# Broadcasting RMS-norm factors in a transposed decoder trunk: two DMAs through a scratch row, and sums as two single products of 132 columns

## The chip, the cores and the metric

One core of a Trainium2 chip runs the kernel. The metric is the device time of one launch in microseconds (us); lower is better. The engines of a core work side by side: TensorE (PE, matrix products, with its weight load PEld), VectorE (DVE), ScalarE (ACT), GpSimd (POOL) and SyncE (SP, which issues most weight transfers). DMA engines move data between HBM, SBUF (on-chip memory, 128 partitions) and the scratch rows in HBM. Products land in PSUM, eight banks of 128 x 512 f32.

## What is computed

A decoder trunk of two layers over 256 tokens of width 1024, all in f32, with a memory of 256 entries. Each layer is FFN, mixer, FFN; layer 0 mixes with an mLSTM, layer 1 with sliding-window attention, and both have four heads of attention to the memory beside it.

```python
def rms_norm(x, g):
    return x * lax.rsqrt(jnp.mean(x * x, axis=-1, keepdims=True) + EPS) * g

mem_kv = rms_norm(mem, mem_norm_g) @ mem_w_kv
for i in range(2):
    x = x + 0.5 * swiglu(rms_norm(x, ffn1_norm_g[i]), ffn1_w_in[i], ffn1_w_out[i])
    proj = rms_norm(x, mix_norm_g[i]) @ (a_w_in, b_w_in)[i]
    x = x + jnp.concatenate([token_mixer(proj), memory_heads(proj)], axis=-1) @ w_out
    x = x + 0.5 * swiglu(rms_norm(x, ffn2_norm_g[i]), ffn2_w_in[i], ffn2_w_out[i])
```

There are seven norms of this kind: one of the memory, and x0 to x5 of the activations. The factor `rsqrt(mean + EPS)` is one number per token.

## The kernel before

**Layout.** Activations lie transposed: channels on the partitions, the 256 tokens along the columns. An activation is four tiles of 128 x 2 x 256. Weights come in tiles of 128 x 1024 (512 KB) by SP's queue into `wr` (five buffers). Each f32 product is made as three faster ones: ACT casts a weight tile to its high part `wh` (L211), DVE subtracts to get the low part `wl` (L212), eight buffers each, and `mm3` issues high x high, low x high and high x low (L225 to L227). A group of 512 output columns fills one PSUM bank.

**Norms.** The gain of a norm is applied before the product (`split_gain` makes `xh` and `xl`, L241 the DVE half), the token factor behind it, so that the products of the next stage run before the factor is known. The squares are added up in `acc` by DVE (L288, folded in L291). `Norm.chain` then makes the factor. Two products on PE with `acc` as the stationary operand and a column of ones as the moving one give the token sums in two columns of a bank (L231 through `mmf`); `rsqrt_cols` makes mean + EPS on DVE (L250) and the power -0.5 on POOL (L251): `rc`, 128 x 2, one token per partition. Where tokens lie along the columns, the factor must stand in every partition: `bcast_rows` (two products with the identity, L231 again) and an ACT copy give `rb`, 128 x 256 (L306), and another `hrb`, half of it. An f32 product takes two passes on PE, so the trace counts four for two products. `rows=False` (the memory norm and x4, the norm before the attention mixer) needs only `rc`.

**Who uses them.** `rb` scales the FFN's hidden units on DVE (L476, followed by a Silu on ACT), in mixer A the output gates (L658), the gate pre-activations (L696, L697) and queries and keys (L754, L757). `hrb` scales the FFN's output (L544, in the last FFN also L533). `rc` scales the columns of groups whose tokens lie on the partitions: through `head_scales` (`qsc`, L364, L365) it goes to `head_norm`, which makes the norm of each head: a square on ACT, a reduce (L374), L377, the power on POOL (L379), L381 and the scaling L383. So in the memory stage and in mixer B, keys and queries wait for `rc`. In the memory stage the second of two key heads is transposed on PE at L236.

**Order.** The program runs memory, FFN, mixer A, FFN, FFN, mixer B, FFN. The order on PE and SP is written out by hand by `Weave`: the main line issues weight products and moves a virtual clock by the price of each; side chains such as `Norm.chain` are spawned with a delay from the table `LAT` and take their turn when the clock has passed it. `LAT['norm_b']` is the delay between the sums and the broadcast, `x0_b` the same for x0. The order on the other engines (DVE, ACT, POOL) is decided by the framework from what becomes ready when; a DMA issued by POOL stands in POOL's queue, and a wait there holds back what is behind it. The late constants, the mask among them, are loaded by POOL's queue (L183 to L190). Mixer A already sends a scratch row through HBM (`gd`, L710, L713), on ACT's queue.

Of the kernel before, what the change touches and what calls it, by code (L numbers as in the profile page):

```python
# [10 lines left out]
F32 = mybir.dt.float32  # L11
# [3 lines left out]
AF = mybir.ActivationFunctionType  # L15
ALU = mybir.AluOpType
# [3 lines left out]
P = 128  # L20
T = 256
D = 1024
# [10 lines left out]
def constants():  # L33
# [16 lines left out]

LAT = dict(pieces=1, norm=7.5, norm_b=4.8, mnorm=2.4, x0=16.0, x0_b=7.5, mkeys=7.2, cross=9.5, cross_s=1.5,
           cross_m=3.7, cross_p=8.7, cross_o=3.0, gates=20.0, scores=2.2, scores_m=8.4, num=6.9, num_r=7.5,
           keys=5.5, keys_d=7.2, query=9.0, head=1.5, head_m=2.5, head_p=9.3, head_o=4.0)


WARM = 18


class Weave:
# [37 lines left out]
def tile_trunk(ctx: ExitStack, tc: tile.TileContext, a, out):  # L99
    nc = tc.nc  # L100
    seq = [0]

    def mk(pool, shape, dt, tag):
        seq[0] += 1
        return pool.tile(shape, dt, tag=tag, name=f"{tag}_{seq[0]}")

    def pool(name, bufs, **kw):
        return ctx.enter_context(tc.tile_pool(name=name, bufs=bufs, **kw))
# [13 lines left out]
    sp = pool("sp", 2)  # L122
# [8 lines left out]
    def act(*args, **kw):  # L131
        ins = nc.scalar.activation(*args, **kw)  # L132
        if args[2] not in (AF.Copy, AF.Square):
            tabled[0] = ins
# [12 lines left out]
    def col():  # L147
        return mk(cp, [P, 16], F32, "col")

    def mo():  # L150
        return mk(pb8, [P, 512], F32, "bank")
# [15 lines left out]
    ident = con[:, C_ID:C_ID + P]  # L167
    maskd = con[:, C_MASK:C_MASK + T]
    ones = mk(cst, [P, 1], F32, "ones")
# [33 lines left out]
    pieces = [1]  # L203
# [26 lines left out]
    def mmf(ps, lhsT, rhs, n, start=True, stop=True):  # L230
        nc.tensor.matmul(ps, lhsT, rhs, start=start, stop=stop, skip_group_check=True)  # L231
        wv.now += max(0.213, n * 0.00182)
# [15 lines left out]
    def rsqrt_cols(dst, src, n, scale):  # L248
        c = col()
        nc.vector.tensor_scalar(c[:, :n], src, scale, EPS, op0=ALU.mult, op1=ALU.add)  # L250
        nc.gpsimd.tensor_tensor(out=dst, in0=c[:, :n], in1=mhalf[:, :n], op=ALU.pow)  # L251

    def bcast_rows(ps, cols):
        for h in range(2):
            mmf(ps[:, h * P:(h + 1) * P], cols[:, h:h + 1].to_broadcast([P, P]), ident, P)

    def pair(x):
        return x.unsqueeze(1).to_broadcast([P, 2, T])


    class Norm:
# [30 lines left out]

        def chain(self, gap=LAT['norm_b']):
            pc = mo()
            for h in range(2):
                mmf(pc[:, h:h + 1], self.acc[:, 0, h * P:(h + 1) * P], ones, 1)
            self.rc = mk(sp, [P, 2], F32, "rc")
            rsqrt_cols(self.rc, pc[:, 0:2], 2, 1.0 / D)
            if not self.rows:
                self.done = True  # L300
                return
            yield gap
            ps = mo()
            bcast_rows(ps, self.rc)
            self.rb = mk(sp, [P, T], F32, "rb")
            nc.scalar.copy(self.rb, ps[:, :T])  # L306
            if self.half:
                self.hrb = mk(sp, [P, T], F32, "hrb")
                act(self.hrb, ps[:, :T], AF.Copy, scale=0.5)
            self.done = True  # L310

        def ready(self):
# [55 lines left out]
    def head_norm(dst, src, n, hsc):  # L368

        hd = src.shape[2] // n  # L370
        sq, v, u = tmp(), col(), col()
        sqv = sq[:, :, :n * hd]
        act(sqv, src, AF.Square)
        nc.vector.tensor_reduce(out=v[:, 0:2 * n].rearrange("p (h m) -> p h m", h=2),  # L374
                                in_=sqv.rearrange("p h (m d) -> p h m d", m=n), axis=AX.X, op=ALU.add)
        for h in range(2):
            nc.vector.tensor_scalar(u[:, n * h:n * h + n], v[:, n * h:n * h + n], hsc[:, h:h + 1], EPS,  # L377
                                    op0=ALU.mult, op1=ALU.add)
        nc.gpsimd.tensor_tensor(out=u[:, 8:8 + 2 * n], in0=u[:, 0:2 * n], in1=mhalf[:, 0:2 * n], op=ALU.pow)  # L379
        for h in range(2):  # L380
            nc.vector.tensor_scalar(v[:, 8 + n * h:8 + n * h + n], u[:, 8 + n * h:8 + n * h + n],  # L381
                                    hsc[:, 2 + h:3 + h], None, op0=ALU.mult)
        tt(out=dst.rearrange("p h (m d) -> p h m d", m=n), in0=src.rearrange("p h (m d) -> p h m d", m=n),  # L383
           in1=v[:, 8:8 + 2 * n].rearrange("p (h m) -> p h m", h=2).unsqueeze(3).to_broadcast([P, 2, n, hd]),
           op=ALU.mult)
# [12 lines left out]
    x0 = Norm(G_F1)  # L398

    def memory():  # L400
# [3 lines left out]
        bank = mo()  # L404
        for i in range(WARM):
            nc.tensor.matmul(bank, idle[:, :P], idle, start=True, stop=True, skip_group_check=True)
# [16 lines left out]
        def keys(gi, kr):  # L423
            nc.scalar.copy(kT[gi], turn(kr))
            return
            yield

        for gi in range(2):
# [13 lines left out]
            norm.fold()  # L442
            wv.spawn(norm.chain(), LAT['mnorm'])
            gv = Group(wkv, 512, mh, ml, rows=True)
# [5 lines left out]
            for i, q in enumerate((first, gr)):  # L450
                kr = tmp()
                head_norm(kr, q.ps, 2, hsc)
                wv.spawn(keys(i, kr), LAT['mkeys'] + 1.5 * i)
        for gi in range(2):
# [7 lines left out]
            if gi == 0:  # L462
                with tc.issue_after(last[0].ins):
                    for c2 in range(4):
                        x0.put(xT[c2])
                wv.spawn(x0.chain(LAT['x0_b']), LAT['x0'])

# [41 lines left out]
    def ffn(x, w_in, w_out, nxt=None, mid=None):  # L509
# [13 lines left out]
        for c2 in range(4):  # L523
            wts = [(kg, w[:, kg[0]:kg[0] + kg[1], c2 * 256:(c2 + 1) * 256]) for kg in KG]
            if nxt is None and c2 == 3:
                wts = [(kg, wtile(src, kg[1])) for kg, src in wts]
                y = tmp()
                for m in range(2):
                    ps = mo()[:, :T]
                    for kg, wt in wts:  # L530
                        products(ps, m, kg, wt, True)
                        yield
                    tt(out=y[:, m], in0=ps, in1=x.hrb, op=ALU.mult)  # L533
                    tt(out=y[:, m], in0=y[:, m], in1=x.xT[c2][:, m], op=ALU.add)
                    nc.scalar.dma_start(out[:, 2 * c2 + m], y[:, m])
                return
            ps = mo()
            for kg, src in wts:
                wt = wtile(src, kg[1])
                for m in range(2):  # L540
                    products(ps[:, m * T:(m + 1) * T], m, kg, wt, m == 0)
                    yield
            t = tmp()
            tt(out=t, in0=halves(ps), in1=pair(x.hrb), op=ALU.mult)  # L544
            xn = unit(F32)
            tt(out=xn, in0=t, in1=x.xT[c2], op=ALU.add)
            if nxt is None:
                nc.scalar.dma_start(out[:, 2 * c2:2 * c2 + 2], xn)
            else:
                nxt.put(xn)  # L550
        wv.spawn(nxt.chain(), LAT['norm'])

# [15 lines left out]
    def cross_spawn(gr, gi, layer, hsc, ys):  # L568
# [4 lines left out]
        def queries():  # L573
# [4 lines left out]
            for m in range(2):  # L578
                wv.spawn(head(m), LAT['cross_s'] + LAT['cross_m'] * m)
            return  # L580
            yield

        def head(m):
            hd, qT = gi * 2 + m, cell[0]
            hi, lo = ys.tiles(4 + gi)
            s = mo()
            for h in range(2):
                mmf(s[:, h * T:(h + 1) * T], qT[:, m, h * P:(h + 1) * P], kT[gi][:, m], T)
            sv = halves(s)
            c = col()  # L590
            nc.vector.tensor_reduce(out=c[:, 2:4], in_=sv, axis=AX.X, op=ALU.max, negate=True)  # L591
            p = unit(F32)
            for h in range(2):
                act(p[:, h], sv[:, h], AF.Exp, bias=c[:, 2 + h:3 + h], accum_out=c[:, 4 + h:5 + h])
            nc.vector.reciprocal(c[:, 6:8], c[:, 4:6])
            tt(out=p, in0=p, in1=c[:, 6:8].unsqueeze(2).to_broadcast([P, 2, T]), op=ALU.mult)
            yield LAT['cross_p']
            tps = mo()
            for mc in range(2):
                for h in range(2):  # L600
                    transpose(tps[:, mc * T + h * P:mc * T + (h + 1) * P], p[:, h, mc * P:(mc + 1) * P])
            pT = tmp()
            nc.scalar.copy(pT, halves(tps))
            yield LAT['cross_o']
            o = mo()
            for mc in range(2):
                mmf(o[:, :T], vM[:, mc, hd * P:(hd + 1) * P], pT[:, mc], T, mc == 0, mc == 1)
            split_plain(o[:, :T], hi[:, m], lo[:, m])
            ys.done.add(8 + hd)
# [39 lines left out]
    def mixer_a(x, nxt):  # L649
# [6 lines left out]
        def og_out(gr):  # L656
            t = unit(F32)
            tt(out=t, in0=gr.ps, in1=pair(x.rb), op=ALU.mult)  # L658
            act(t, t, AF.Sigmoid)
            og.append(t)  # L660
# [366 lines left out]
```

## Time and profile before

| | |
|---|---|
| median of three runs | 1012.32 us (1012.27 to 1013.65) |
| profiled execution | 1012.23 us, span of its trace 1010.4 us |
| granted TensorE clock | 1.000 |
| DMA | 182.70 MB, mean 181 GB/s |
| DVE weight splits `wl` (L212) | x347, 414.7 us busy |
| ACT weight casts `wh` (L211) | x347, 356.8 us busy |
| POOL | 32 instructions, 35.7 us busy |

A row of the timeline view reads: start in us, length in us, engine, line, operation, what is written from what, shapes, number of instructions run together; in brackets the idle time of the engine before it and what ended that. L225 and so on are lines of the kernel before. A group row of the page reads: line, engine, operation, tiles, shapes and count, then busy us and mean ns of one, then idle time of the engine before them with what ended most of it.

### The profile page before, as it was taken

How to read it: one execution, taken by the hardware profiler on the slowest of the kernel's cores; microseconds unless marked ns; L12 is line 12 of the kernel's file. 1: busy time of each engine (PE TensorE's matmuls, PEld its weight loads, DVE VectorE, ACT ScalarE, POOL GpSimd, SP SyncE). 2: the span in 40 equal slices, each digit the busy share in tenths (PEclk: the TensorE clock that was granted, in tenths of full speed). 3: DMA queues.
4: the chain of work that ended last, by engine and by line, in shares of the span. 5: the costliest groups of instructions: out<-in, count | busy, mean ns of one | idle time of the engine just before them, and what ended most of it. 6: DMA issues, size and time to landing. Idle time of an engine off the chain costs nothing.

```text
span 1010.4 us, 20624 instructions
## 1 busy us (share of the span) xinstructions
PE 998.5 (99%) x8594; PEld 980.2 (97%) x8594; DVE 655.5 (65%) x1063; ACT 519.5 (51%) x764; POOL 35.7 (4%) x32
## 2 busy tenths in 40 slices
PE   8999999999999999999999999999999999999998
PEld 7999999999999999999999999999987899999998
DVE  6866665577856676665558666656787766666551
ACT  7754445446656554444445544544557754454440
POOL 1200000000001000000000000000121000000000
PEclk9999999999999999999999999999999999999999
DMA  9776656666644566665676666567541347666550
GB/s 308 242 245 200 192 180 185 199 183 179 184 139 133 167 210 195 200 189 170 192 206 205 189 191 201 173 197 198 182 131 66 100 131 220 198 189 185 188 170 21
DMA packets 173204, 182.70 MB, mean 181 GB/s; under 512 B 7124, under 2 KB 168328, under 8 KB 173112
## 3 DMA queue, kind: packets, MB, share of 16 engines
q1 hardware_dynamic: 171872, 179.60, 58.3%
q10 hardware_dynamic: 1016, 1.58, 0.5%
q8 instruction: 67, 1.10, 0.5%
q0 software_dynamic: 224, 0.22, 0.2%
q14 instruction: 25, 0.20, 0.1%
HBM read 180.32 MB, written 1.05 MB: 180 GB/s over the span
## 4 chain that ended last, share of the span: by engine, by line
PE 94%; DVE 3%; ACT 1%; DMA 1%; POOL 0%; issue 0%; SPq 0%; ACTq 0%
PE bank L225 30%; PE bank L226 30%; PE bank L227 30%; PE bank L231 2%; PE bank L236 1%; ACT u L132 1%; DVE wl L212 1%; DMA wr<-in_mem_w_kv_dram 1%; PE bank L961 1%; POOL col L379 0%; DVE col L930 0%; DVE u L383 0%; DVE col L591 0%; PE bank L925 0%; DVE u L946 0%
## 5 line engine op out<-in xcount | busy, mean ns | idle before, releaser
L212 DVE TENSOR_TENSOR wl<-wr,wh 128x1024 fp32r<-128x1024 f32 (+1 forms) x347 | 414.7, 1196 | 279.8 <-ACT wh L211 279.0
L211 ACT CAST wh<-wr 128x1024 fp32r<-128x1024 f32 (+1 forms) x347 | 356.8, 1031 | 393.1 <-PE bank L226 368.9
L225 PE MATMUL bank<-xh,wh 128*128 128x256 f32 x1544 | 429.1, 278 | 0.0
L226 PE MATMUL bank<-xl,wh 128*128 128x256 f32 x1544 | 426.8, 276 | 0.0
L227 PE MATMUL bank<-xh,wl 128*128 128x256 f32 x1544 | 426.8, 276 | 0.0
L226 PEld LDWEIGHTS bank<-xl,wh 128*128 128x128 f32 x1544 | 290.3, 188 | 0.1
L225 PEld LDWEIGHTS bank<-xh,wh 128*128 128x128 f32 x1544 | 290.0, 188 | 0.1
L227 PEld LDWEIGHTS bank<-xh,wl 128*128 128x128 f32 x1544 | 289.9, 188 | 0.0
L225 PE MATMUL bank<-u,wh 128*128 128x256 f32 x896 | 249.3, 278 | 0.0
L226 PE MATMUL bank<-u,wh 128*128 128x256 f32 x896 | 247.6, 276 | 0.0
L227 PE MATMUL bank<-u,wl 128*128 128x256 f32 x896 | 247.6, 276 | 0.0
L225 PEld LDWEIGHTS bank<-u,wh 128*128 128x128 f32 x896 | 168.2, 188 | 1.9 <-issue 1.7
L226 PEld LDWEIGHTS bank<-u,wh 128*128 128x128 f32 x896 | 168.4, 188 | 0.1
L227 PEld LDWEIGHTS bank<-u,wl 128*128 128x128 f32 x896 | 168.3, 188 | 0.0
L225 PE MATMUL bank<-wh,xh 128*128 128x256 f32 x208 | 59.7, 287 | 0.0
L226 PE MATMUL bank<-wl,xh 128*128 128x256 f32 x208 | 57.9, 278 | 0.0
L227 PE MATMUL bank<-wh,xl 128*128 128x256 f32 x208 | 57.9, 278 | 0.0
L476 DVE TENSOR_TENSOR t<-bank,rb 128x256 f32<-128x256 f32 x88 | 36.6, 420 | 7.3 <-PE bank L227 7.3
L225 PEld LDWEIGHTS bank<-wh,xh 128*128 128x128 f32 x208 | 39.1, 188 | 0.5 <-issue 0.3
L226 PEld LDWEIGHTS bank<-wl,xh 128*128 128x128 f32 x208 | 39.1, 188 | 0.1
L227 PEld LDWEIGHTS bank<-wh,xl 128*128 128x128 f32 x208 | 39.0, 187 | 0.0
L479 DVE TENSOR_TENSOR t<-t,bank 128x256 f32<-128x256 f32 x88 | 32.7, 412 | 1.8 <-ACT t L132 1.8
(171 smaller groups left out, 657.5 us busy)
## 6 DMA issues: line engine op xcount, KB each, us to landing
wr<-in_ffn_w_in_dram SPq DMA_DIRECT2D x176, 512.0 KB, 3.6
wr<-in_ffn_w_out_dram SPq DMA_DIRECT2D x80, 512.0 KB, 3.5
wr<-in_a_w_in_dram SPq DMA_DIRECT2D x28, 512.0 KB, 3.9
wr<-in_b_w_in_dram SPq DMA_DIRECT2D x14, 512.0 KB, 4.6
wr<-in_a_w_out_dram SPq DMA_DIRECT2D x12, 512.0 KB, 3.3
wr<-in_b_w_out_dram SPq DMA_DIRECT2D x12, 512.0 KB, 3.4
wr<-in_ffn_w_out_dram SPq DMA_DIRECT2D x16, 256.0 KB, 2.8
wr<-in_mem_w_kv_dram SPq DMA_DIRECT2D x7, 512.0 KB, 8.0
```

The source lines that it names most:

```text
L132: ins = nc.scalar.activation(*args, **kw)
L211: last[0] = nc.scalar.copy(hi[:, i * n:(i + 1) * n], src[:, i * n:(i + 1) * n])
L212: tt(out=lo[:, i * n:(i + 1) * n], in0=src[:, i * n:(i + 1) * n], in1=hi[:, i * n:(i + 1) * n].bitcast(F32), op=ALU.subtract)
L225: nc.tensor.matmul(ps, wh, xh, start=start, stop=False, skip_group_check=True)
L226: nc.tensor.matmul(ps, wh, xl, start=False, stop=False, skip_group_check=True)
L227: nc.tensor.matmul(ps, wl, xh, start=False, stop=stop, skip_group_check=True)
L231: nc.tensor.matmul(ps, lhsT, rhs, start=start, stop=stop, skip_group_check=True)
L236: nc.tensor.transpose(ps, src, ident[:k, :k])
L476: tt(out=t[:, m], in0=ps[m][:, :T], in1=x.rb, op=ALU.mult)
L479: tt(out=t[:, m], in0=t[:, m], in1=ps[m][:, T:], op=ALU.mult)
L961: nc.tensor.matmul(o[es[e], cs], vr[:, i, js], pTs[e][:, src], start=i == 0, stop=i == 1, skip_group_check=True)
```

## The change

The two products of sums no longer run side by side. Each has 132 columns of ones as its moving operand, writes 132 columns of its own half of the bank, and a delay `norm_h` of 2.0 on the virtual clock stands between them; `rsqrt_cols` reads one column of each half. In the order on PE, 24 weight matmuls lie between the two. This holds for all seven norms. For the five norms with rows, the two products with the identity and both ACT instructions are gone: POOL writes `rc` to a row of a new scratch tensor in HBM and reads it back into all 128 partitions as `rb`; POOL's queue waits for the first before the second. `hrb` is made by DVE from `rb`. The delays `norm_b` and `x0_b` become 11.0. SP's order stays as it was, and so does the order of the rest on PE. The order on DVE shifts in places: in the start-up two weight splits move ahead of L250, and eight in place of six stand ahead of the second key head (L383); in mixer B one split moves ahead of L250.

```diff
-LAT = dict(pieces=1, norm=7.5, norm_b=4.8, mnorm=2.4, x0=16.0, x0_b=7.5, mkeys=7.2, cross=9.5, cross_s=1.5,
+LAT = dict(pieces=1, norm=7.5, norm_h=2.0, norm_b=11.0, mnorm=2.4, x0=16.0, x0_b=11.0, mkeys=7.2, cross=9.5, cross_s=1.5,
...
+SUMS = 132
...
-    def bcast_rows(ps, cols):
-        for h in range(2):
-            mmf(ps[:, h * P:(h + 1) * P], cols[:, h:h + 1].to_broadcast([P, P]), ident, P)
-
...
+    turned = []
...
         def chain(self, gap=LAT['norm_b']):
             pc = mo()
             for h in range(2):
-                mmf(pc[:, h:h + 1], self.acc[:, 0, h * P:(h + 1) * P], ones, 1)
+                mmf(pc[:, h * 256:h * 256 + SUMS], self.acc[:, 0, h * P:(h + 1) * P], ones.to_broadcast([P, SUMS]), SUMS)
+                if h == 0:
+                    yield LAT['norm_h']
             self.rc = mk(sp, [P, 2], F32, "rc")
-            rsqrt_cols(self.rc, pc[:, 0:2], 2, 1.0 / D)
+            rsqrt_cols(self.rc, pc.rearrange("p (h t) -> p h t", h=2)[:, :, 0], 2, 1.0 / D)
             if not self.rows:
                 self.done = True
                 return
+            rd = a["rd"][len(turned)]
+            turned.append(self)
+            self.rb = mk(sp, [P, T], F32, "rb")
+            nc.gpsimd.dma_start(rd.rearrange("(h p) -> p h", p=P), self.rc)
+            nc.gpsimd.dma_start(self.rb, rd.partition_broadcast(P))
             yield gap
-            ps = mo()
-            bcast_rows(ps, self.rc)
-            self.rb = mk(sp, [P, T], F32, "rb")
-            nc.scalar.copy(self.rb, ps[:, :T])
             if self.half:
                 self.hrb = mk(sp, [P, T], F32, "hrb")
-                act(self.hrb, ps[:, :T], AF.Copy, scale=0.5)
+                nc.vector.tensor_scalar(self.hrb, self.rb, 0.5, None, op0=ALU.mult)
             self.done = True
...
     aps["gd"] = nc.dram_tensor("gd_dram", (4, T), F32, kind="Internal").ap()
+    aps["rd"] = nc.dram_tensor("rd_dram", (5, T), F32, kind="Internal").ap()
```

## The prediction

> **What bounds the kernel now.** I read the page first, for who is busy and which engine the last chain follows.
>
> ```profile
> PE 998.5 (99%) x8594; PEld 980.2 (97%) x8594; DVE 655.5 (65%) x1063; ACT 519.5 (51%) x764; POOL 35.7 (4%) x32
> ...
> PE 94%; DVE 3%; ACT 1%; DMA 1%; POOL 0%; issue 0%; SPq 0%; ACTq 0%
> ...
> L212 DVE TENSOR_TENSOR wl<-wr,wh 128x1024 fp32r<-128x1024 f32 (+1 forms) x347 | 414.7, 1196 | 279.8 <-ACT wh L211 279.0
> L211 ACT CAST wh<-wr 128x1024 fp32r<-128x1024 f32 (+1 forms) x347 | 356.8, 1031 | 393.1 <-PE bank L226 368.9
> ```
>
> TensorE (PE) is the bound: 99% busy, 94% of the chain. The other lines say how the rest follows it: VectorE (DVE) waits for the ScalarE (ACT) casts, 279.0 us of 279.8, and those wait for PE to free a weight buffer, 368.9 us of 393.1. So there are two ways to change the time: give PE more or fewer passes, or make PE wait at one of the few places where it is fed just in time. The windows view shows that in the first FFN it never waits:
>
> ```profile
> 40.00:220.00 180.00, 180.00 (x1588) 180.00 (x1587) 117.29 (x149) 91.15 (x110) 2.31 (x2) 1.00 0.67 203
> ```
>
> (Columns: stretch and length, then busy us of PE, PE weight load, DVE, ACT, POOL, then granted clock, DMA share, GB/s.) The clock is 1.00, so no term below depends on it.
>
> **PE's own work.** PE's instructions overlap, so a price is the distance between starts. PE's timeline around a pair of sums, a broadcast pair and a group of four 256-column passes:
>
> ```profile
> 45.67 0.28 PE L227 MATMUL bank<-xh,wl 128*128 128x256 f32 x1
> 45.78 0.50 PE L231 MATMUL bank<-ones,acc 128*128 128x1 f32 x4
> ...
> 46.34 0.28 PE L226 MATMUL bank<-xl,wh 128*128 128x256 f32 x1
> 46.46 0.28 PE L227 MATMUL bank<-xh,wl 128*128 128x256 f32 x1
> ...
> 54.59 0.28 PE L227 MATMUL bank<-xh,wl 128*128 128x256 f32 x1
> 54.71 0.61 PE L231 MATMUL bank<-con,rc 128*128 128x128 f32 x4
> ...
> 55.27 0.28 PE L226 MATMUL bank<-xl,wh 128*128 128x256 f32 x1
> ...
> 260.85 0.28 PE L227 MATMUL bank<-xh,wl 128*128 128x256 f32 x1
> 260.96 1.02 PE L231 MATMUL bank<-kT,u 128*128 128x256 f32 x4
> ...
> 261.94 0.28 PE L226 MATMUL bank<-xl,wh 128*128 128x256 f32 x1
> ```
>
> A weight matmul follows the last after 0.11 to 0.12. From L227 to the next L226 lie two such distances (0.23) and the price of what is pushed in between. An f32 product is two passes, so x4 is two products. The sums pair costs 46.34 - 45.67 - 0.23 = 0.44; the broadcast pair 55.27 - 54.59 - 0.23 = 0.45; the four 256-column passes 261.94 - 260.85 - 0.23 = 0.86. So 128 more columns cost (0.86 - 0.45)/4 = 0.10 a pass, and a group has a fixed part of 0.45 - 4 x 0.10 = 0.04 or so. One column is no cheaper than 128.
>
> - Removed: five broadcast pairs (norms x0, x1, x2, x3, x5), 5 x 0.45 = -2.25.
> - Added: each sums pair becomes two single products of 132 columns, 24 weight matmuls apart in PE's order. A single costs 0.04 + 2 x 0.10 x 132/128 = 0.25, two 0.50, which is +0.06 a norm. For six norms +0.35; the seventh, the memory's, stands in the start-up below. No single product stands in this trace. From below two singles cost the pair (0); from above each costs as much as a whole pair, 6 x 0.44 = +2.65. I take +0.35, as the passes are alike.
>
> Together **-1.9**. The freed ACT copies (five rb, four hrb, under 0.4 each) count for nothing, since ACT waits for PE anyway; of the hrb, now on DVE, the same holds, with 35% of DVE free.
>
> **The second sum comes later.** 24 matmuls of 0.117 and one more fixed part: every L250 and rc, the norm factors, come 24 x 0.117 + 0.04 = 2.85 later. In the FFN norms (x0, x2, x3, x5) nothing needs rc before rb. In three stages it matters.
>
> **Start-up (memory norm).** Here the heads of the memory keys hang on rc. DVE, POOL (GpSimd) and PE in the timeline:
>
> ```profile
> 24.55 0.50 PE L231 MATMUL bank<-ones,acc 128*128 128x1 f32 x4
> ...
> 25.09 0.16 DVE L250 TENSOR_SCALAR col<-bank 128x2 f32<-128x2 f32 x1 [0.97 <-PE bank L231]
> ...
> 26.09 0.16 DVE L364 SCALAR_TENSOR_TENSOR qsc<-rc 128x2 f32<-128x2 f32 x1 [0.25 <-POOL rc L251]
> ...
> 26.90 1.22 DVE L212 TENSOR_TENSOR wl<-wr,wh 128x1024 fp32r<-128x1024 f32 x1
> ...
> 27.08 1.91 POOL L379 TENSOR_TENSOR col<-col,mhalf 128x4 f32<-128x4 f32 x1 [1.02 <-DVE col L377]
> ...
> 36.27 0.36 DVE L381 TENSOR_SCALAR col<-col,qsc 128x2 f32<-128x2 f32 x2 [0.90 <-POOL col L379]
> ...
> 37.67 0.68 DVE L383 TENSOR_TENSOR t<-bank,col 128x512 f32<-128x512 f32 x1
> ...
> 38.50 0.63 PE L236 MATMUL bank<-con,t 128*128 128x128 f32 x4
> ```
>
> The second head key (L383) is done at 38.35 and PE transposes it at 38.50: 0.15 of slack. After the change L250 runs at 25.09 + 2.85 = 27.95. While it waits DVE does what the new order puts ahead of it: the last xl, the first square reduce, and two weight splits that stood behind it. But the new order also puts two later splits ahead of the second head key, so six lie between L250 and it, as before. DVE's walk in the new order, with the durations above: qsc 28.95 (1.0 after L250, as before), a split to 30.25, L377 to 30.5, POOL's 1.91 to 32.4 (a split beside it), L381, a split to 33.8, first head key 34.4, reduce 35.0, a split to 36.15, L377 36.4, a split to 37.55 and POOL to 38.5 side by side, L381 38.8, a split to 39.95, second head key 40.6. PE gets it at 40.65, not 38.50: **+2.15**. Lower bound +0.5, if the six splits fall wholly into POOL's waits; upper +3.0, if none of the work that is put ahead shortens the chain. Nothing later gives it back, as PE is full from there on.
>
> **FFN norms: rb by two transfers.** rb was on ACT at 55.74; now it goes POOL power, write to the row, wait for it on POOL's queue, read back.
>
> ```profile
> 55.74 0.36 ACT L306 COPY rb<-bank 128x256 f32<-128x256 f32 x1
> ...
> u<-in_mask_dram POOLq DMA_DIRECT2D x1, 192.0 KB, 5.5
> ...
> u<-gd_dram ACTq DMA_DIRECT2D x2, 256.0 KB, 5.0
> ...
> posi<-in_positions_dram POOLq DMA_DIRECT2D x1, 1.0 KB, 5.7
> ```
>
> (Last number: us from issue to landing.) posi has the write's shape, 256 elements of four bytes; the mask's issue has rb's size and queue. At most 5.7 + 5.5 after rc; so in x0 DVE stands at its first use of rb (L476) until about 62 to 65, and ACT's Silu behind it. Behind them wait the splits. Eight pairs of weight buffers hold eight times 24 matmuls of 0.113, 21 us of PE's work, and ACT waits for PE to free one, so most are full: some 16 us of cover. I cost it at 0; a wait beyond that cover would go straight to PE. The mask's DMA now queues behind x0's two on POOL; its reader is a late constant, far off: 0.
>
> **Mixer A (x1).** DVE reaches L658, which reads rb, soon after rc:
>
> ```profile
> 224.34 0.16 DVE L250 TENSOR_SCALAR col<-bank 128x2 f32<-128x2 f32 x1 [0.25 <-PE bank L231]
> ...
> 232.25 1.88 DVE L658 TENSOR_TENSOR u<-bank,rb 128x512 f32<-128x512 f32 x3
> ...
> 232.25:242.64 10.39, 10.39 (x94) 10.39 (x94) 6.51 (x9) 7.63 (x10) 0.00 (x0) 1.00 0.64 170
> ...
> 253.35 0.69 DVE L383 TENSOR_TENSOR u<-bank,col 128x512 f32<-128x512 f32 x1
> ...
> 257.79 0.38 PE L236 MATMUL bank<-con,u 128*128 128x128 f32 x2
> ...
> 224.69 0.72 POOL L251 TENSOR_TENSOR rc<-col,mhalf 128x2 f32<-128x2 f32 x1 [173.03 <-DVE col L250]
> ```
>
> rc comes at 224.69 + 0.72 + 2.85 = 228.3. DVE idles 10.39 - 6.51 = 3.9 us until 242.64, so rb by 236.1 costs nothing even on DVE. The first matmul that waits on DVE's later work is at 257.79; its operand is done at 254.04, 3.75 earlier. So PE feels little before rb = 239.9. By the rows rb lands between 228.3 + 2.5 + 4 = 234.8 (two reads of gd took 5.0 each, issue included; a 4 KB write should need half) and 228.3 + 5.7 + 5.5 = 239.5. I take the middle, 237, and **0**; up to +3 beyond it.
>
> **Mixer B (x4, no rows).** rc feeds a long chain of head norms:
>
> ```profile
> 719.58 0.16 DVE L250 TENSOR_SCALAR col<-bank 128x2 f32<-128x2 f32 x1 [0.44 <-PE bank L231]
> ...
> 740.11 0.68 DVE L591 TENSOR_REDUCE col<-bank 128x2 f32<-128x512 f32 x1
> ...
> 741.74 0.69 ACT L132 ACTIVATE u<-bank,gqk 128x512 f32<-128x512 f32 x1
> ...
> 742.47 1.13 PE L231 MATMUL bank<-kT,u 128*128 128x256 f32 x4 [1.45 <-ACT u L132]
> ```
>
> PE already waits 1.45 here, for ACT's u, done at 742.43, and ACT for L591. Each us that L591 is late goes to PE. L250 moves to 722.45; of the six splits between L250 and L591 one now stands ahead of L250 (-1.15), and small reorderings (a reduce ahead of L250) take 0.4: 2.85 - 1.15 - 0.4 = **+1.3**. Bounds 0 (more splits fall into POOL's waits) and +2.85.
>
> **Sum.** -1.9 + 2.15 + 0 + 0 + 1.3 = +1.55. On the profiled run's own 1012.23 (its span is 1010.4; 1.8 lies around it) that is **1013.8**. The median shown is 1012.32, 0.1 above. What a measurement can tell from no change is 0.2%, 2.0 us: faster is below 1010.3, slower above 1014.35.
>
> **The rivals.**
> - *A, all of it hidden.* DVE fits the splits into POOL's waits, and only PE's gain is left: 1012.23 - 1.9 = 1010.3. For it: 35% of DVE is free. Against it: 0.15 of slack at 38.50 and a wait of 1.45 at 742.47, with 2.85 to bear.
> - *D, one of the two stalls only:* 1012.23 - 1.9 + 2.15 = 1012.5, or with +1.3, 1011.6. For it: DVE's order in either stage leaves room for a us.
> - *B, slower: rb too late in mixer A.* DVE's queue stands at L658 until rb has come; it decides from rb = 239.9 on. For it, POOL beside a busy DVE:
>
> ```profile
> 49.34 1.75 POOL L251 TENSOR_TENSOR rc<-col,mhalf 128x2 f32<-128x2 f32 x1 [13.11 <-DVE col L250]
> ```
>
>   That is 1.03 more than the 0.72 at 224.69, for the same instruction. If rc and each DMA issue are held up as long beside a split, rb lands at 239.5 + 3 x 1.03 = 242.6, 2.7 beyond the point: 1013.8 + 2.7 = 1016.5. Against it: DVE, once stuck at L658, holds nothing up any more, and the queues are less full than at the start, where posi was read. The Trainium skill, "SBUF — State Buffer", section "SBUF: two separate sides", speaks for it: a DMA issued from GpSimd has its descriptors written by GpSimd's cores, which a VectorE instruction can lock out of a shared port, and about 620 ns became about 3100. By that figure two issues would lose an estimated 5 us; the trace agrees for POOL's power, 0.72 against 1.75, and no run here shows an issue beside DVE in that state.
> - *C, slower: a single product costs as much as the pair* (a switch of operand type at each group, not its passes, is what is paid): +2.65 in place of +0.35, 1016.1. Against it: the 256-column group's 0.86 grows with the columns.
>
> **How the numbers follow.** Forecast (both stalls, rb in time) 0.38, over 1012.4 to 1015.2; A 0.16; D 0.12; B 0.18; C 0.16. Faster than 0.2%: two thirds of A and a little of D, 0.13. Within: 0.23 of the forecast, 0.05 of A, 0.10 of D, 0.04 of B and C: 0.42. Slower: 0.15 of the forecast, 0.16 of B, 0.14 of C: 0.45. The range goes from just below A, 1010.0, to above B, 1017.0.
>
> **What would show it.** In the changed profile: the transpose of the second head key near 40.65 (right) or still near 38.5 (A); the wait at the first scores of mixer B near 743.8 less what PE has gained by then; the distance over a single sum 0.25 (right) or 0.44 (C) above 0.23; L658 in mixer A waiting for the DMA of rb, with or without a PE gap near 258 to 271 (B); the L476 of each FFN waiting for rb while PE shows no gap. A PE gap in an FFN would make the prediction wrong in the part costed at nothing.

## The result, and the profile after

The changed kernel takes 1024.76 us (median of 4 runs, 1022.12 to 1025.17) against 1012.30 before: a ratio of 1.0116, 95% interval 1.0101 to 1.0131. It is slower by 12 us. The prediction said 1013.8, range 1010.0 to 1017.0.

The page of the changed kernel, to be read beside the first lines of the prediction:

```profile
PE 1000.0 (98%) x8574; PEld 981.6 (96%) x8574; DVE 652.3 (64%) x1067; ACT 516.4 (51%) x755; POOL 38.6 (4%) x42
...
PE 89%; DVE 4%; DMA 2%; ACT 2%; POOL 1%; issue 1%; SPq 0%; ACTq 0%; DVEq 0%; POOLq 0%
```

PE's share of the chain fell from 94% to 89%, and DMA, DVE and ACT took it over: somewhere PE now waits for a transfer through the other engines. Its timeline shows where (start, length, engine and line; in brackets the idle time before):

```profile
41.94 0.63 PE L237 MATMUL bank<-con,t 128*128 128x128 f32 x4 [2.11 <-DVE t L386]
...
267.81 1.11 PE L237 MATMUL bank<-con,u 128*128 128x128 f32 x4 [7.87 <-DVE u L386]
...
273.63 0.33 PE L228 MATMUL bank<-xh,wl 128*128 128x256 f32 x1
...
756.06 0.78 PE L226 MATMUL bank<-wh,xh 128*128 128x256 f32 x1
```

The first is the second head key of the start-up. The second is mixer A, the place of rival B, with 7.87 us of idle PE. The matmul at 273.63 stood at 260.85 before, 12.8 us earlier. The windows view of that stretch (columns as in the prediction):

```profile
259.00:267.80 8.80, 0.94 (x9) 0.74 (x7) 7.80 (x16) 6.27 (x10) 1.94 (x1) 0.76 0.59 170
267.80:274.00 6.20, 6.18 (x29) 6.18 (x30) 5.16 (x11) 1.69 (x3) 1.91 (x1) 0.52 0.82 265
274.00:280.00 6.00, 6.00 (x45) 5.58 (x43) 4.39 (x8) 3.86 (x11) 0.00 (x0) 1.00 0.84 244
```

PE does almost nothing for 8 us, and then runs 6 us at a granted clock of 0.52 of full speed. What it waited for is told by POOL's timeline and then DVE's:

```profile
230.16 0.72 POOL L252 TENSOR_TENSOR rc<-col,mhalf 128x2 f32<-128x2 f32 x1 [164.69 <-DVE col L251]
231.18 0.75 POOL L307 DMA_DIRECT2D rd_dram<-rc  x1 [0.30 <-POOL rc L252]
242.17 0.56 POOL L308 DMA_DIRECT2D rb<-rd_dram  x1 [10.24 <-DMA rd_dram<-rc]
```

```profile
247.94 0.69 DVE L661 TENSOR_TENSOR u<-bank,rb 128x512 f32<-128x512 f32 x1 [13.13 <-DMA rb<-rd_dram]
...
267.07 0.69 DVE L386 TENSOR_TENSOR u<-bank,col 128x512 f32<-128x512 f32 x1
```

The write of 1 KB holds POOL's queue for 10.24 us; rb is there at 247.9; DVE stands 13.13 us; the operand that PE wants is done at 267.76. The trace's records of the write's own packets all lie between 232.5 and 233.2, and the signals of its landing come from 236.3 to 241.9: the time passes behind the packets, and what happens in it is not shown.

In the first FFN DVE stands almost as long, 11.79 us, and PE has no gap there:

```profile
69.31 0.29 DVE L312 TENSOR_SCALAR hrb<-rb 128x256 f32<-128x256 f32 x1 [11.79 <-DMA rb<-rd_dram]
```

The same weight matmul in the two profiled executions, from PE's timelines, gives the account of the 12.2 us between 1012.23 and 1024.43:

| place | before | changed | later by |
|---|---|---|---|
| ahead of the first sum | 22.67 | 24.35 | 1.68 |
| behind the second head key | 38.88 | 42.32 | 3.44 |
| behind x0's broadcast | 55.27 | 57.95 | 2.68 |
| behind x1's broadcast | 230.47 | 232.48 | 2.01 |
| first of mixer A behind the gap | 258.14 | 268.58 | 10.44 |
| ahead of the first scores of mixer A | 260.85 | 273.63 | 12.78 |
| behind x2's broadcast | 364.42 | 376.51 | 12.09 |
| behind x3's broadcast | 545.06 | 556.48 | 11.42 |
| in the sums of x4 | 719.40 | 730.60 | 11.20 |
| behind the first scores of mixer B | 743.25 | 756.06 | 12.81 |
| nine matmuls later | 744.50 | 758.34 | 13.84 |
| behind the next wait of mixer B | 756.41 | 769.25 | 12.84 |
| late in mixer B | 762.64 | 775.33 | 12.69 |
| behind x5's broadcast | 840.56 | 852.57 | 12.01 |
| last | 1006.26 | 1018.26 | 12.00 |

The first 1.68 arise before any changed instruction of PE: between 14 and 18 us the granted clock was 0.57 in this execution and 1.00 in that of before. Other kernels here show the same in some executions and not in others (1.00 with x1 broadcast by PE, 0.62 in the mix below), so it isn't counted to the change.

Mixer B also holds a stretch at half clock, behind a wait that had grown from 1.45 to 2.14 us:

```profile
754.76 1.86 PE L232 MATMUL bank<-kT,u 128*128 128x256 f32 x4 [2.14 <-ACT u L133]
...
755.00:758.40 3.40, 3.40 (x14) 3.05 (x14) 3.23 (x6) 2.39 (x8) 0.00 (x0) 0.50 0.12 22
```

It makes PE 1.55 us later by 758.34 (0.52 in the products of the first row, then 1.03). At 763.91 PE then has no longer the wait of 1.05 us that stood there before (751.08 in the trace of before), so a third of it stays.

### The profile page after: what moved, and what is told of

The parts are those of the page before. It is cut to its first block, busy times and chain, and to the rows that moved or that the text cites. A ratio compares the mean times of both kernels' runs of the same rounds, so it can differ in the third digit from the quotient of the medians.

```text
span 1022.4 us, 20585 instructions
## 1 busy us (share of the span) xinstructions
PE 1000.0 (98%) x8574; PEld 981.6 (96%) x8574; DVE 652.3 (64%) x1067; ACT 516.4 (51%) x755; POOL 38.6 (4%) x42
## 4 chain that ended last, share of the span: by engine, by line
PE 89%; DVE 4%; DMA 2%; ACT 2%; POOL 1%; issue 1%; SPq 0%; ACTq 0%; DVEq 0%; POOLq 0%
PE bank L226 28%; PE bank L227 28%; PE bank L228 28%; PE bank L232 2%; PE bank L237 1%; POOL col L382 1%; DVE wl L213 1%; DMA rd_dram<-rc 1%; ACT u L133 1%; DMA wr<-in_mem_w_kv_dram 1%; PE bank L964 1%; DMA rb<-rd_dram 1%; ACT wh L212 0%; PE bank L928 0%; DVE col L377 0%
## 5 line engine op out<-in xcount | busy, mean ns | idle before, releaser
L133 ACT ACTIVATE t<-t 128x512 f32<-128x512 f32 x44 | 27.7, 629 | 53.7 <-DVE t L479 53.7
```

## The experiments

**x1 by PE.** The changed kernel with one norm put back.

```diff
-        x1, x2, x3 = Norm(G_MIX, half=False), Norm(G_F2), Norm(G_F1 + 8)
+        x1, x2, x3 = Norm(G_MIX, half=False, pe=True), Norm(G_F2), Norm(G_F1 + 8)
```

> Theory (mixer A carries the loss): in the changed kernel the write of rc to the row took 10.2 us to land, rb came at 247.9 instead of 239.9 or earlier, PE stood 8.15 us and then ran 2.35 us behind at a low granted clock. With the norm x1 alone broadcast by PE again, about 10.8 of the 12.2 us go and one broadcast pair (0.5) comes back: 1013 to 1014.5, no PE gap over 1 us between 42 and 740 us. Rival (the other four transfers or the split sums cost PE time everywhere): still 1018 or more.

1012.89 us (ratio to before 1.0004, 0.9989 to 1.0019). The windows view of mixer A has PE full at full clock:

```profile
220.00:300.00 80.00, 80.00 (x659) 78.70 (x659) 55.62 (x97) 46.50 (x80) 4.55 (x3) 1.00 0.55 170
```

That is just below the expected 1013 to 1014.5. One transfer in one stage carries nearly all of the loss; the other four are covered. The rival falls.

**Sums side by side again**, one column each, all broadcasts by DMA (the edit below); and **split sums only**, where the sums stay as changed and all five norms take the branch `pe=True`.

```diff
-                mmf(pc[:, h * 256:h * 256 + SUMS], self.acc[:, 0, h * P:(h + 1) * P], ones.to_broadcast([P, SUMS]), SUMS)
-                if h == 0:
-                    yield LAT['norm_h']
+                mmf(pc[:, h * 256:h * 256 + 1], self.acc[:, 0, h * P:(h + 1) * P], ones, 1)
```

> Sums together again as two products of one column, all five rows still by two DMAs. Theory: rc comes 2.85 us earlier in each norm, so the gap in mixer A shrinks from 8.15 to about 5.3 us, the gap of 2.3 us before the second key head and the 1.4 us of mixer B go: 1017 to 1019. Rival (the delay of the sums has no part in mixer A's gap, or the start's): above 1022. Rival (only the sums cost): 1012 to 1013.

> All five broadcasts by PE and ACT as before, the sums still two single products of 132 columns, 24 matmuls apart. Theory: start-up +2, mixer B +1.4, mixer A +0 to +1, PE's own work about 0: 1014 to 1016. Rival (what stops mixer A is the late sums rather than the DMA): 1020 or more.

1041.61 us (1.0277, 1.0244 to 1.0310) and 1041.57 us (1.0273, 1.0234 to 1.0313). Both lie over 20 us above what the theory gave. They fall among the times of the rivals (above 1022, 1020 or more), but not by what the rivals name: with split sums alone mixer A has no wait of PE at all, so the late sums do not stop it. With the sums side by side the wait in mixer A is shorter, and the start-up's is gone, yet the run loses 29. Of the 5.3 us by which the wait is shorter, the theory gave 2.85; 1.7 is a faster landing of the write, for which POOL waited 8.57 us here:

```profile
267.05 0.66 PE L237 MATMUL bank<-con,u 128*128 128x128 f32 x4 [2.54 <-DVE u L384]
```

No further wait of PE behind the start is that long. The windows view of the first FFN, one row each of the kernel before and of this one, shows it:

```profile
60.00:220.00 160.00, 160.00 (x1414) 160.00 (x1414) 101.07 (x128) 78.11 (x93) 0.00 (x0) 1.00 0.64 189
```

```profile
60.00:220.00 160.00, 160.00 (x1361) 160.00 (x1360) 101.08 (x132) 78.08 (x92) 1.11 (x2) 1.00 0.61 192
```

PE is full and at clock 1.00 in both, but does 1361 matmuls in place of 1414. 160 us / 1414 is 113.2 ns, 160 / 1361 is 117.6. The groups view gives the mean length of one as 276 ns in the changed kernel and 281 ns with the sums side by side, for the same instruction:

```profile
L228 PE MATMUL bank<-xh,wl 128*128 128x256 f32 x296 | 81.7, 276 | 0.0
```

```profile
L228 PE MATMUL bank<-xh,wl 128*128 128x256 f32 x282 | 79.2, 281 | 0.0
```

So back-to-back matmuls have two cadences, 113.3 and 117.8 ns (averages of starts over some 30), and each is kept until a product of another kind comes between. In every kernel here with acc at its usual place, a pair of sums that came while PE ran at the fast cadence put it on the slow one. A broadcast pair switched it, either way, but for x0's with split sums, which came on the slow cadence and stayed there. In the kernel before, that was a slow stretch of 6 to 9 us between each pair of sums and its broadcast; windows view of before, behind x0's sums and behind its broadcast:

```profile
47.00:54.00 7.00, 7.00 (x62) 7.00 (x61) 4.54 (x6) 4.08 (x4) 2.31 (x2) 1.00 0.98 311
57.00:64.00 7.00, 7.00 (x64) 7.00 (x63) 6.43 (x13) 4.88 (x7) 0.00 (x0) 1.00 0.71 230
```

With no broadcast behind it (sums side by side) the slow cadence lasts through the FFN; with split sums, which leave the cadence of an FFN as it is, the broadcast pairs of x2, x3 and x5 throw PE out of the fast one (x0's FFN was on the slow one ahead of its sums). Split sums do not always keep the fast one: behind x4's, in mixer B, PE went from 113.3 to 117.8 ns in the changed kernel as well.

**The write on ACT's queue.**

```diff
-            nc.gpsimd.dma_start(rd.rearrange("(h p) -> p h", p=P), self.rc)
+            nc.scalar.dma_start(rd.rearrange("(h p) -> p h", p=P), self.rc)
```

> The changed kernel with the write of rc issued on ACT's hardware queue, the read back still on POOL's. Theory Q (POOL's software queue makes the write slow): it lands in 1.5 to 3 us, as gd's 4 KB write did in 1.3, rb at about 240, the gap in mixer A is below 1 us: 1013 to 1015. Theory E (256 elements of four bytes are slow on any queue): it still lands in 8 to 10 us, the gap is 6 to 8 us: 1021 to 1025.

1020.66 us (1.0070, 1.0048 to 1.0091). The DMA view (last number: median us to landing) has the write on POOL's queue in the changed kernel and on ACT's here:

```profile
rd_dram<-rc POOLq DMA_DIRECT2D x5, 1.0 KB, 10.2
```

```profile
rd_dram<-rc ACTq DMA_DIRECT2D x5, 1.0 KB, 9.1
```

That is no clear share for the queue: POOL's own writes of this form have a median of 9.4 with the sums side by side and 9.1 in the mix below. Theory Q falls; of theory E stands that the write is slow on either queue, while the gap and the time came out a little below its ranges. PE's idle in mixer A fell by 2.8 us with rb, which DVE got at 245.16:

```profile
265.05 1.12 PE L237 MATMUL bank<-con,u 128*128 128x128 f32 x4 [5.11 <-DVE u L386]
```

**Mix:** memory norm, x1 and x4 as before the change, the four FFN norms as changed; then the same with the FFN sums side by side at 132 columns, and apart at one column.

```diff
+    MODES = {'mem': ('two1', ''), 'x4': ('two1', ''), 'x1': ('two1', 'pe'),
+             'x0': ('one132', 'dma'), 'x2': ('one132', 'dma'), 'x3': ('one132', 'dma'), 'x5': ('one132', 'dma')}
...
-                if h == 0:
+                if h == 0 and sums[:3] == "one":
                     yield LAT['norm_h']
```

(`two` is side by side, `one` apart, the number is the columns.)

> Memory norm, x1 and x4 as in the kernel before (pair of one-column sums, PE broadcast for x1); x0, x2, x3, x5 as in the changed kernel. Theory K (two cadences of the weight matmuls, 113.3 and 117.8 ns apart, which products in between switch; a pair of one-column sums leaves the slow one, single sums of 132 columns the fast one): each of the four norms gains 0.7 us and no gap is added: 1009 to 1010. Rival (the transfers or the late sums cost something in every norm): 1011.5 or more.

> As mix, but the sums of x0, x2, x3 and x5 are two products of 132 columns side by side. Theory K with the reading that a pair of products does it, whatever its columns: each of these FFNs runs at 117.8 ns to its end, some 1500 matmuls x 4.5 ns = 6.5 to 7 us each, 1034 to 1040. Rival (the width of 132 keeps the fast cadence): 1009 to 1010.

> As mix, but the single sums of x0, x2, x3 and x5 have one column. Theory K with the reading that only the distance between the products matters: 1009 to 1010. Rival (one column leaves the slow cadence, whether single or not): 1034 to 1040. In between if single products of one column switch it only at some places.

1009.70 us (0.9974, 0.9965 to 0.9983), 1031.04 us (1.0184, 1.0170 to 1.0197) and 1009.65 us (0.9982, 0.9965 to 0.9999; one of ten runs took 1018.8). The mix is faster than both kernels: what the change holds for the FFN norms is a gain. In these FFN norms it is the distance between the two sums that keeps the fast cadence: single sums of 1 and of 132 columns do so alike, and a pair of 132 columns on the fast cadence loses it like a pair of one column. The pair of 132 columns lost 21 instead of the 24 to 30 expected, as x3's pair, which came on the slow cadence, switched back to the fast one; with one column it had not.

**Four ways of writing the row**, one in each FFN of the mix: 256 elements of 4 bytes, 128 of 8, 512 of 4, and two rows of 512 bytes after a transpose on PE.

```diff
+                nc.gpsimd.dma_start(rd[:T].rearrange("(p h) -> p h", p=P), self.rc)
...
+                nc.gpsimd.dma_start(rd.rearrange("(h p) -> p h", p=P), rc4)
...
+                nc.tensor.transpose(pt[:2, :P], self.rc, ident)
+                nc.scalar.copy(rt, pt[:2, :P])
+                nc.gpsimd.dma_start(rd[:T].rearrange("(h p) -> h p", p=P), rt)
```

> As mix, but the row is written in four ways: x0 256 elements of 4 bytes, x2 128 of 8 bytes (with one more DVE copy behind the read), x3 512 of 4 bytes, x5 two rows of 512 bytes (turned on PE, copied by ACT). Theory E (the number of elements sets the time of the write): it lands about 10, 5 to 6, 18 to 20 and 1.5 to 2.5 us after issue. Rival (a fixed wait of the queue behind the weight loads): 9 to 11 in all four. Time as mix, within 2 us, unless an FFN waits.

The time was 1038.25 us. The DMA view answers for the writes (rc x2 is x0 and x2 together, 10.3 and 5.6 us):

```profile
rd_dram<-rc POOLq DMA_DIRECT2D x2, 1.0 KB, 7.9
...
rd_dram<-rc POOLq DMA_DIRECT2D x1, 2.0 KB, 10.0
...
rd_dram<-rt POOLq DMA_DIRECT2D x1, 1.0 KB, 3.0
```

512 elements of 4 bytes took no longer than 256, against theory E's 18 to 20: their number alone does not set the time, and their size is what is left (256 elements of 8 bytes were not tried). The rival, one wait for all, falls too. The 28 us beyond the mix were not expected. Behind the sums of all four FFNs PE now ran at the slow cadence, with the same instructions on PE up to x0's sums. What else differs is SBUF: the extra tiles moved acc, which the sums load as stationary operand, by 3136 bytes in its partition. Two runs tell whether that is it: **the mix with an unused tile** that moves acc likewise, and **the four ways with the extra tiles behind acc**.

```diff
+    mk(sp, [P, 392], F32, 'pad')
```

```diff
+    zp = pool("zp", 2)
...
-                rc4 = mk(sp, [P, 4], F32, "rc4")
+                rc4 = mk(zp, [P, 4], F32, "rc4")
```

> As mix, with one unused tile of 3136 bytes a partition ahead of acc, so that acc stands in SBUF where it stood in the run with four ways of writing; no instruction differs. Theory L (where acc lies in SBUF decides whether its products switch the weight matmuls to 117.8 ns): about 1036, slow from the first sum of x0. Rival (the other instructions of that kernel did it): 1009 to 1010.5.

> The four ways of writing the row again, with their extra tiles behind all others, so that acc stands where it stands in mix. Theory L: fast cadence through the four FFNs, 1008 to 1012. Rival: 1036 to 1039 again. The four writes land 10, 5.6, 10 and 3 us after issue, as they did.

1037.73 us (1.0251, 1.0231 to 1.0272) and 1017.54 us. The windows row of the padded mix:

```profile
60.00:220.00 160.00, 160.00 (x1360) 160.00 (x1360) 98.59 (x130) 76.89 (x91) 1.11 (x2) 1.00 0.64 187
```

An unused tile costs 28 us. It moves all that is allocated behind it; of that, the sums read acc alone. Theory L holds for the first three FFNs of the second run; in the last, where the transpose of rc stands between the weight matmuls, it went slow again (117.8 ns), which is most of the 7.8 us it lies above the mix.

**The row turned on PE, and the row of 8-byte elements**, each in all five norms of the changed kernel, by the edits of the four ways, with the extra tiles behind acc.

> The changed kernel, but rc is turned on PE (one transpose), copied by ACT, and the row written as two pieces of 512 bytes, in all five norms. Theory W (mixer A's gap is the landing of the write of 4-byte elements): the write lands in 3 us, rb at about 228.5 + 1.5 + 3 + 4.5 = 238 to 240, mixer A's gap under 1 us and no drop of the granted clock there: 1012 to 1014 while the FFNs keep 113.3 ns. Rival (the gap comes from the POOL queue as such): gap over 5 us, above 1019.

> The changed kernel, but the row is written as 128 elements of 8 bytes, and DVE puts the columns in order behind the read. Theory W: the write lands in 5.6 us, rb 4.1 us earlier than in the changed kernel (with the copy): gap of mixer A about 4 instead of 8.15 us: 1018 to 1020. Rival (5.6 was one lucky landing): gap 7 or more, 1023 or more.

The writes, then PE's windows in mixer A with turned rows, and DVE and PE with 8-byte elements:

```profile
rd_dram<-rt POOLq DMA_DIRECT2D x5, 1.0 KB, 2.6
```

```profile
rd_dram<-rc POOLq DMA_DIRECT2D x5, 1.0 KB, 6.2
```

```profile
232.00:262.00 30.00, 30.00 (x265) 29.98 (x264) 18.60 (x32) 16.72 (x24) 3.79 (x4) 1.00 0.65 181
262.00:275.00 13.00, 13.00 (x104) 12.54 (x103) 11.18 (x21) 6.99 (x14) 1.91 (x1) 1.00 0.85 241
```

```profile
243.12 0.29 DVE L338 COPY rb<-rw 128x256 f32<-128x256 f32 x1 [6.11 <-DMA rw<-rd_dram]
```

```profile
263.35 0.33 PE L238 MATMUL bank<-con,u 128*128 128x128 f32 x1 [1.21 <-DVE u L425]
```

With turned rows neither a gap nor a drop of the clock is left in mixer A: theory W holds. The time, 1032.69 us (1.0207, 1.0190 to 1.0224), misses, because the single transpose switched three of the four FFNs to 117.8 ns. The 8-byte row gave 1018.27 us (1.0059, 1.0039 to 1.0079) and an idle of 1.21 where 4 was expected. x1's write landed in 4.3 us here, not in the 5.6 counted on. Of its time, 1.5 us are half clock behind the second head key (0.51 between 42.6 and 46.0), which the changed kernel did not have there; that the time lies in the expected range is in part luck.

**PE kept busy in the gap.** The drop of the clock costs the changed kernel 12.78 - 10.44 = 2.34 us behind the gap, and 0.4 in the four transposes at its end (0.77 us to the next start in place of 0.35). Here 46 products of constants, whose results nothing reads, stand on PE ahead of these transposes.

```diff
+        for i in range(n):
+            nc.tensor.matmul(ps[:, :3 * P], identb, maskb, start=True, stop=True, skip_group_check=True)
```

> The changed kernel with 46 bf16 products of constants (no wait, results overwritten) on PE ahead of the transpose that waited 8.15 us in mixer A, some 7.5 us of work. Theory G (PE's idle time there lowers the granted clock for the next 6 us): the clock stays 1.00 from 259 to 274 and the 2.35 us behind the gap go, the gap itself is filled and not shortened: 1021 to 1022.5. Rival (the drop comes from something else that happens at that time, the transfers or DVE's load): the clock drops as before, 1024 to 1025.

1021.03 us (1.0076, 1.0060 to 1.0093), and the windows:

```profile
259.00:267.80 8.80, 8.80 (x60) 5.82 (x59) 7.24 (x15) 4.77 (x6) 3.57 (x2) 1.00 0.70 223
267.80:274.00 6.20, 6.20 (x51) 5.94 (x50) 5.78 (x11) 2.76 (x7) 0.28 (x1) 1.00 0.71 211
```

With the same stretch of waiting filled, PE does 51 matmul records where it did 29, at a clock of 1.00: its idle time brought on the drop. The Trainium skill, "TensorE: Matmul & The Clock Gate", in its part on the HAM clock gate, has the gate pass half of the pulses after an idle window of about 3.4 us; 0.52 behind 7.87 us of idle agrees. A drop also stood behind a shorter wait: behind the 2.14 us in mixer B the clock was 0.50 for 3.4 us in the changed kernel, while it stayed at 1.00 behind the same wait with x1 broadcast by PE. That the wait brought it on is not shown there. The rows of that execution, wait and clock:

```profile
743.45 1.13 PE L232 MATMUL bank<-kT,u 128*128 128x256 f32 x4 [2.14 <-ACT u L133]
...
743.00:747.00 4.00, 3.56 (x26) 3.45 (x27) 3.92 (x8) 2.99 (x9) 0.00 (x0) 1.00 0.12 25
```

## Why the prediction was wrong, by its steps

- **The step that failed** is mixer A: "I take the middle, 237, and **0**; up to +3 beyond it", from bounds of 234.8 and 239.5. It was 247.9 (of which 2.0 is what every instruction there was late). So this term, put at 0, measured +10.8: 7.9 of waiting and 2.8 of low clock. The nearest row by shape, posi, is a read of 4-byte elements (5.7 us); the write of such elements took 10.2, and both ends of the bound lay below it. The mechanism had been named as rival B, with the right place; its price, 2.7, came from POOL held up beside DVE, and that did not happen: rc took 0.72 and the two issues 0.75 and 0.56. The rule on the shared port in the Trainium skill, "SBUF — State Buffer", section "SBUF: two separate sides", is not what acted here: the first issue, beside a split, took 0.75 and not the 3.1 us of the prediction's citation. The Trainium skill, "DMA: Bandwidth & Descriptors", section "Specifications", sets 512 bytes as the least transfer at full rate; the order of 2.6, 6.2 and 10.2 us for 512, 8 and 4 bytes goes that way.
- **The point from which it decides** was near: rb 239.9 on the clock of before, with "3.9 us" of DVE's idle time to spend. From rb (247.91 by landing) to PE's operand (267.76) it took 19.85 us; by the 21.8 of before less 3.9 it would have been 17.9. About half of that idle time could not be spent, as DVE still waited for ACT (0.50 and 1.72 us) and POOL (0.93). The same 19.85 gives 265.0 from the ACT run's 245.16 and 263.3 from the 8-byte run's 243.41; PE went on at 265.05 and 263.35.
- **The clock** was read as 1.00 and dropped as a term. It is a result of PE's waits: about 2.8 of mixer A's 10.8.
- **PE's own work**, -1.9 predicted, was -3.5 by the starts in the two traces (0.76, 0.67, 0.69, 0.67 and 0.69 for x0, x1, x2, x3 and x5; x5's from 12.69 late in mixer B to 12.00; x4's sums took off 0.22 and put back 0.23). A single sum was sized right, 0.23 against 0.25; PE's timeline:

```profile
49.10 0.28 PE L228 MATMUL bank<-xh,wl 128*128 128x256 f32 x1
49.22 0.39 PE L232 MATMUL bank<-ones,acc 128*128 128x132 f32 x2
...
49.56 0.28 PE L227 MATMUL bank<-xl,wh 128*128 128x256 f32 x1
```

  That is 0.46 less two distances of 0.115. What was missed is that the old sums and broadcasts set the price of the matmuls between them: 72 of them in x0 and 48 in the others, at 4.5 ns each, are 0.32 and 0.22 us a norm, beside the 0.45 of the broadcast pair.
- **The start-up** was right: +1.76 by the table (3.44 - 1.68) against +2.15, with the gap at 41.94 where 40.65 stood, 1.68 of it by the clock at 14 us. **Mixer B** came out at +1.3, as predicted, but by luck: from 11.58 ahead of the first scores to 12.84 behind, of which the wait itself is 0.69 (2.14 against 1.45), half clock 1.55, and a later wait that went away -1.0. With x1 broadcast by PE, where the clock stayed at 1.00, the same wait cost 0.7. The FFNs and the mask were rightly costed at nothing.
- Rival C falls by the 0.23. A and D described parts that did happen, without the one that decided.

Terms as measured: -3.5 (norms) + 1.8 (start-up) + 10.8 (mixer A) + 1.3 (mixer B) + 1.7 (clock at the start) = 12.1, against 12.2.

## What to carry to other kernels

A broadcast through HBM is paid by the landing of its small write; take its price from a row of the same direction and element size, or bound it far higher, and use it only where enough buffered work stands behind the waiting engine: in the first FFN here it covered a wait of 11.8 us, in mixer A it did not cover 13.1. When a kernel is bound by back-to-back matmuls, count matmuls per us stage by stage before and after: a few odd products, or a tile's address, can move every later one by 4%. Where a change helps in most places and hurts in one, put back the one: the mix is 0.26% faster than the kernel before.

## What the runs showed of the hardware

- Two cadences of the same matmuls at the same granted clock: 113.3 and 117.8 ns, kept for 180 us and more. Products of another kind between them can switch it. On the fast one, a pair of sums side by side brought the slow one every time, with acc at its usual place. Sums 24 matmuls apart kept the fast one ahead of the FFNs and of mixer A, but not in mixer B, and with their stationary operand moved by 3136 bytes they lost it ahead of the FFNs as well. Why is open; acc was tried at two places only.
- A write of 4-byte elements to HBM landed after 9.1 to 10.2 us (medians of three kernels on POOL's queue; 9.1 from ACT's), of 8-byte elements after 6.2, of two 512-byte rows after 2.6; 512 elements of 4 bytes took no longer than 256.
- 8 us without matmuls were followed by 6 us at half the clock (0.52); with PE kept busy they were not. Behind a wait of 2.1 us the clock was at half for 3.4 us in some executions and not in others.
